# Conditioning of a two-layer trunk: its accumulator moves to a PSUM bank in sets of 512 columns, and its sums over partitions to TensorE and ScalarE

## The chip, the cores and the metric

The kernel runs on one core of a Trainium2 chip. The metric is the device time of one execution in microseconds; before the change it is 2387.78 us, the median of three runs (2386.66 to 2390.29). The profile is of one execution on that core.

## The reference

A trunk of two layers works on 256 tokens of width 2048, in float32. Each layer has a token mixer (layer 0: a gated unit that mixes positions within chunks of 128; layer 1: attention with a forget gate) and a dense layer of hidden width 5632. Each of the four parts gets a shift, a scale and a gate from the condition vector c:

```
c_act = silu(c)
for i in range(DEPTH):
    mod = c_act @ ada_w[i] + ada_b[i]
    sh1, sc1, g1, sh2, sc2, g2 = jnp.split(mod, N_MOD, axis=-1)
    h = modulate(rms_norm(x, norm_mix_g[i]), sh1, sc1)
    ...
    x = x + g1[:, None, :] * y
    h = modulate(rms_norm(x, norm_ffn_g[i]), sh2, sc2)
    x = x + g2[:, None, :] * swiglu_ffn(h, ffn_w_gate[i], ffn_w_up[i], ffn_w_down[i])
```

The product with ada_w, (2, 2048, 6 x 2048), is a vector times a matrix of 201 MB in all: the conditioning, which this change is about.

## The kernel before

Weights come in chunks of 1 MB (4 k-tiles of 128 rows x 512 columns, wchunk) into one of five raw buffers, which the conditioning shares. ScalarE casts half of a chunk to the high part hi (L259), and VectorE or GpSimd subtracts it from raw to give the low part lo (L263). In layer 0 up to the gate and up products every second low part is GpSimd's, later every sixth. TensorE multiplies hi and lo with the split operand, three products for each pair of tiles (mm_a, L300 to L304, for results with channels on partitions; mm_b, L316 to L318, for results by token). VectorE adds partial results from PSUM into SBUF: v at L510, u at L525, the gate and up sums gu at L696, the residual xT at L444.

The conditioning is a product with one row, so VectorE makes it, with ada_w's rows on partitions. A set is 1024 columns: shift and scale of 4 blocks of 128, or 8 blocks of a gate. It comes in 8 chunks of 1 MB (ada_chunk), each of 2 k-tiles; each k-tile is one VectorE step over 1024 columns, acc = raw x cact + acc, with acc in SBUF (L171 for the first, L176 for the other 15):

```
nc.vector.scalar_tensor_tensor(
    out=acc, in0=raw[:, k, :], scalar=cact[:, kt : kt + 1], in1=acc,
    op0=ALU.mult, op1=ALU.add,
)
```

After the eighth chunk ada_sum adds over the 128 partitions. For the six sets of layer 0's mixer TensorE transposes the eight blocks into PSUM (L197) and ScalarE sums each over its row (L203). For the other 18 sets VectorE does it: four transposes within blocks of 32 (L212), four reductions (L213), a product with the matrix fold on TensorE (L218) and four adds into mod (L222). From the scale comes acol (L225), from acol and rstd the operand hA (modulate, L412 to L421).

The order is set in two steps. In the program, pump calls ada_next after each weight chunk at a rate (1.5 to 0.95 in layer 0's mixer, 1.0 and 0.78 up to the gate and up products of the first dense layer, then 0.5), and need calls it until a set that is wanted next is done. From this the tile scheduler fixes the order on each engine when the kernel is built; each engine then takes its instructions in that order. From the dense layers on, a conditioning step also stands behind the last low part but one of VectorE (paced).

PSUM has eight banks: six in the pool psm for the products (banks), two in psx for everything else (misc): transposes, norms, the spatial weights pre, the scores of attention.

Of the kernel before, what the change touches and what calls it, by code (L numbers as in the profile page):

```python
# [8 lines left out]
F32 = mybir.dt.float32  # L9
F32R = mybir.dt.float32r  # L10
AF = mybir.ActivationFunctionType
ALU = mybir.AluOpType
# [4 lines left out]
P = 128  # L17
# [11 lines left out]
# Vectors of the conditioning, in the order of their columns.  # L29
# [4 lines left out]
def trunk_kernel(  # L34
# [107 lines left out]
    ada_v = [ada_w[i].rearrange("(kt p) (v n) -> p kt v n", p=P, n=D) for i in range(2)]  # L142
    # A set is SH and SC of 4 blocks, or 8 blocks of a gate; its product comes in 8 chunks of 1 MB.
    ada_acc = {}
    # The last low parts that VectorE makes; once paced, its part of a chunk goes behind them.
    lo_last, paced = [], []

    def ada_chunk(layer, half, b0, q):
        """Chunk q of 8 of SH and SC of 4 blocks from b0, or of 8 blocks of the gate."""
        raw = rawp.tile([P, 4, 512], F32, tag="raw", name="raw")  # L150
        raw = raw.rearrange("p a b -> p (a b)").rearrange("p (k w) -> p k w", k=2)
        ks = slice(2 * q, 2 * q + 2)
        if b0 < KT:
            for v in range(2):
                nc.sync.dma_start(
                    out=raw[:, :, 512 * v : 512 * v + 512],
                    in_=ada_v[layer][:, ks, 3 * half + v, P * b0 : P * b0 + 512],
                )
        else:
            c0 = P * (b0 - KT)  # L160
            nc.sync.dma_start(out=raw, in_=ada_v[layer][:, ks, 3 * half + 2, c0 : c0 + 1024])
        if q == 0:
            ada_acc[0] = accp.tile([P, 1024], F32, tag="acc", name="acc")
        acc = ada_acc[0]
        for k in range(2):
            kt = 2 * q + k
# [13 lines left out]
        if q == 7:  # L180
            ada_sum(layer, half, b0, acc)

    def ada_sum(layer, half, b0, acc):
        """The sums over the partitions: by TensorE and ScalarE while the loads and VectorE hold
        the time; else within blocks of 32 by the transposing copy, then over the four blocks
        by a product with fold[p, q] = (p = q mod 32)."""
        red = small.tile([P, 32], F32, tag="red", bufs=2, name="red")
        pair = b0 < KT
        key = (layer, half, b0)
        mv = mod[layer].rearrange("p (v n) -> p v n", n=16)[:, 3 * half : 3 * half + 3, :]  # L190
        dst = mv[:, 0:2, b0 : b0 + 4] if pair else mv[:, 2:3, b0 - KT : b0 - KT + 8]
        if key in by_pe:
            for h in range(2):
                pt = misc()
                for b in range(4):
                    bs = slice(P * b, P * b + P)
                    nc.tensor.transpose(  # L197
                        out=pt[:, bs], in_=acc[:, 512 * h + P * b : 512 * h + P * b + P],
                        identity=ident,
                    )  # L200
                for b in range(4):
                    junk = tmp.tile([P, T], F32, tag="t", bufs=5, name="junk")
                    nc.scalar.activation(  # L203
                        out=junk[:, :P], in_=pt[:, P * b : P * b + P], func=AF.Identity,
                        accum_out=red[:, 4 * h + b : 4 * h + b + 1],
                    )
            src = red[:, :8].rearrange("p (v n) -> p v n", v=dst.shape[1])
            nc.vector.tensor_add(out=dst, in0=dst, in1=src)
        else:
            for a in range(4):  # L210
                tr = tmp.tile([P, T], F32, tag="t", bufs=5, name="tr")
                nc.vector.transpose(out=tr, in_=acc[:, T * a : T * a + T])  # L212
                nc.vector.tensor_reduce(  # L213
                    out=red[:, 8 * a : 8 * a + 8],
                    in_=tr.rearrange("p (c i) -> p c i", i=32), axis=AX.X, op=ALU.add,
                )
            pt = misc()[:, :32]
            nc.tensor.matmul(pt, lhsT=fold, rhs=red, start=True, stop=True)  # L218
            src = pt.rearrange("p (v n a) -> p v n a", v=dst.shape[1], a=4)
            for a in range(4):  # L220
                r = slice(32 * a, 32 * a + 32)
                nc.vector.tensor_add(out=dst[r], in0=src[r, :, :, a], in1=dst[r])  # L222
        if pair:
            s = slice(b0, b0 + 4)
            nc.vector.scalar_tensor_tensor(  # L225
                out=acol[layer][half][:, s], in0=mv[:, 1, s], scalar=1.0,
                in1=(gain_mix, gain_ffn)[half][layer][:, s], op0=ALU.add, op1=ALU.mult,
            )
        ready.add(key)

    by_pe = {(0, 0, b) for b in range(0, 32, 4)}
    ready = set()
    ada_todo = [
        (layer, half, b0, q)
        for layer in range(2) for half in range(2) for b0 in (0, 4, 8, 12, KT, KT + 8)
        for q in range(8)
# [13 lines left out]
    def need(layer, half, b0):  # L250
        """The chunks up to the set from k-tile b0 (-1: the gate) are in the program."""
        while (layer, half, b0) not in ready:
            ada_next()

# [12 lines left out]
    # What the splits of the next half chunks don't overtake, and the engine of their low parts.  # L267
# [18 lines left out]
    def mm_a(ps, parts, xs, first, last, fused=True, order="p"):  # L286
        """Transposed results of four blocks, [hi x (hi | lo)] and [lo x hi], or their sum."""
# [20 lines left out]
    def mm_b(ps, parts, xs, first, last, fused=True, order="p"):  # L308
        """Results by token of 512 columns, for the two blocks of tokens."""
# [15 lines left out]
    def proj(  # L325
# [3 lines left out]
        """head: the operand is still being made, by prep if given; tail: the results are waited  # L329
        for; also: other work, by chunk."""  # L330
# [13 lines left out]
    def summed(ps):  # L344
        """hi x hi + lo x hi + hi x lo of a bank, [P, T]."""
        s = tmp.tile([P, T], F32, tag="t", bufs=5, name="us")
        nc.scalar.copy(out=s, in_=ps[:, T:])
        nc.vector.tensor_add(out=s, in0=ps[:, 0:T], in1=s)
        return s

# [14 lines left out]
    def rsqrt(y, ms, n, width):  # L365
        """y = (ms / n + EPS) ** -0.5 with a Newton step after the table's value."""
# [16 lines left out]
    def load_table(func, after):  # L383
        """The table of an activation of a later column, while nothing waits for it."""
        nc.scalar.activation(out=rstd[:, 0:1], in_=after, func=func)

    def norm(sq, stt, square):
        """After the last block of the residual: rstd."""
# [6 lines left out]
    def head_start(first, prep):  # L395
        """The first operand after a norm goes before the splits of the second chunk."""
# [3 lines left out]
    def split_into(dst, src):  # L400
        """src [P, T] as dst = (hi | lo)."""
# [3 lines left out]
    def modulate(h, k0, n, a, sh):  # L405
        """The k-tiles of a chunk, on VectorE in the order written: no wait but the first."""
# [605 lines left out]
```

## Time and profile before

| | |
|---|---|
| median of 3 runs | 2387.78 us (2386.66 to 2390.29) |
| span of the profiled execution, first to last instruction | 2387.4 us |
| TensorE products / weight loads busy | 2250.8 us (94%) / 2030.7 us (85%) |
| VectorE busy | 1829.0 us (77%) |
| ScalarE busy | 1072.8 us (45%) |
| GpSimd busy | 682.2 us (29%) |
| moved from and to HBM | 605.63 MB, mean 254 GB/s |

Of the profiled execution the trace has the span and no other time; it stands 0.4 us below the median. Busy time is the time in which an engine has an instruction at work. A share over the whole span hides that the stages have different limits, so the rows below are read by stage. TensorE's matmuls are pipelined and their ends are modelled, so its busy time is not its rate.

The stages of the program, by TensorE's products in the trace: the first operand is ready at 47 us; layer 0's u and v products to 287 us, its output projection and norm to 409; gate and up of the first six groups of the dense layer to 733, the rest of it to 1205; attention to 1512, its output projection to 1609; gate and up of layer 1 to 1900, the rest to the end.

### The profile page before, as it was taken

The numbers are of one execution on the slowest core, as the hardware profiler recorded it, in microseconds if no ns is written. First come the engines' busy times: TensorE is split into PE (matmuls) and PEld (weight loads), VectorE is DVE, ScalarE is ACT, GpSimd is POOL, SyncE is SP. The second block draws the span as 40 slices with busy tenths as digits, with TensorE's granted clock in tenths as the row PEclk, the third lists the DMA queues.
The fourth block names the chain that finished last, engine by engine and source line by source line (L and its number), as shares of the span: only waits on it lengthen the run. The fifth ranks groups of instructions, "written<-read, shape, count | busy, mean of one in ns | idle before, by whom it ended". The sixth has DMA issues, their size and how long they took to land.

```text
span 2387.4 us, 36384 instructions
## 1 busy us (share of the span) xinstructions
PE 2250.8 (94%) x14333; PEld 2030.7 (85%) x14333; DVE 1829.0 (77%) x2340; ACT 1072.8 (45%) x1609; POOL 682.2 (29%) x385
## 2 busy tenths in 40 slices
PE   5898887999989999999989999999999999999998
PEld 3777777999878888888978888889999988888887
DVE  7899997899997778677688767767798974444464
ACT  4434643533344344544444444445444533444443
POOL 2343354444462111212221121231113511122221
PEclk8999998999999999999999999999999999999999
DMA  9889785978867788788758777667778775555552
GB/s 372 290 275 317 248 313 198 349 282 286 290 237 250 282 285 287 260 296 290 254 178 281 265 261 272 218 241 247 266 268 284 241 261 184 190 191 180 194 177 89
DMA packets 290703, 605.63 MB, mean 254 GB/s; under 512 B 13634, under 2 KB 13762, under 8 KB 290274
## 3 DMA queue, kind: packets, MB, share of 16 engines
q1 hardware_dynamic: 290242, 603.14, 73.1%
q8 instruction: 112, 1.84, 0.3%
q14 instruction: 59, 0.48, 0.1%
q0 software_dynamic: 288, 0.16, 0.0%
q10 hardware_dynamic: 2, 0.01, 0.0%
HBM read 601.15 MB, written 2.11 MB: 253 GB/s over the span
## 4 chain that ended last, share of the span: by engine, by line
PE 71%; DVE 22%; issue 4%; DMA 2%; ACT 1%; POOL 0%; SPq 0%; DVEq 0%; ACTq 0%; POOLq 0%
PE mm L300 30%; PE mm L304 22%; DVE acc L176 8%; PE mm L302 6%; PE mm L303 6%; DVE lo L263 5%; DVE gu L696 2%; PE mm L317 1%; PE mm L318 1%; PE mm L316 1%; DVE hA L421 1%; DVE m L403 1%; DMA raw<-in_ada_w_dram 1%; ACT hi L259 1%; DVE v L510 1%
## 5 line engine op out<-in xcount | busy, mean ns | idle before, releaser
L259 ACT CAST hi<-raw 128x1024 fp32r<-128x1024 f32 x752 | 781.2, 1050 | 906.1 <-PE mm L300 501.4
L263 DVE TENSOR_TENSOR lo<-raw,hi 128x1024 fp32r<-128x1024 f32 x560 | 733.2, 1315 | 373.1 <-ACT hi L259 371.3
L304 PE MATMUL mm<-hA,lo 128*128 128x256 f32 x3584 | 987.2, 285 | 19.8 <-DVE lo L263 19.3
L263 POOL TENSOR_TENSOR lo<-raw,hi 128x1024 fp32r<-128x1024 f32 x192 | 510.6, 2661 | 1345.0 <-ACT hi L259 1228.8
L304 PEld LDWEIGHTS mm<-hA,lo 128*128 128x128 f32 x3584 | 685.3, 193 | 31.8 <-DVE lo L263 22.2
L300 PE MATMUL mm<-hA,hi 128*128 128x512 f32 x1792 | 623.8, 397 | 8.9 <-DVE hA L421 8.9
L176 DVE SCALAR_TENSOR_TENSOR acc<-raw,cact,acc 128x1024 f32<-128x1024 f32 x360 | 553.9, 1539 | 6.4 <-DMA raw<-in_ada_w_dram 3.8
L302 PE MATMUL mm<-hA,hi 128*128 128x256 f32 x1792 | 509.8, 290 | 43.4 <-DVE gu L696 25.4
L303 PE MATMUL mm<-hA,hi 128*128 128x256 f32 x1792 | 510.3, 287 | 0.0
L300 PE MATMUL mm<-m,hi 128*128 128x512 f32 x1248 | 432.9, 397 | 0.0
L300 PEld LDWEIGHTS mm<-hA,hi 128*128 128x128 f32 x1792 | 333.1, 188 | 81.1 <-issue 8.4
L302 PEld LDWEIGHTS mm<-hA,hi 128*128 128x128 f32 x1792 | 348.4, 196 | 52.0 <-DVE gu L696 29.1
L304 PE MATMUL mm<-m,lo 128*128 128x256 f32 x1408 | 382.1, 281 | 2.4 <-DVE lo L263 2.4
L303 PEld LDWEIGHTS mm<-hA,hi 128*128 128x128 f32 x1792 | 352.0, 196 | 0.2
L304 PEld LDWEIGHTS mm<-m,lo 128*128 128x128 f32 x1408 | 266.2, 189 | 8.9 <-DVE lo L263 3.2
L300 PEld LDWEIGHTS mm<-m,hi 128*128 128x128 f32 x1248 | 231.8, 188 | 49.1
L696 DVE TENSOR_TENSOR gu<-mm,gu 128x256 f32<-128x256 f32 x288 | 110.8, 414 | 30.2 <-PE mm L304 29.7
L444 DVE SCALAR_TENSOR_TENSOR xT<-mm,mod,xT 128x256 f32<-128x256 f32 x176 | 75.0, 476 | 48.6 <-PE mm L304 48.6
L317 PE MATMUL mm<-lo,hA 128*128 128x512 f32 x256 | 101.9, 399 | 5.6 <-DVE lo L263 5.6
L316 PE MATMUL mm<-hi,hA 128*128 128x512 f32 x256 | 99.4, 403 | 3.6 <-ACT hA L416 3.6
L318 PE MATMUL mm<-hi,hA 128*128 128x512 f32 x256 | 99.7, 392 | 0.0
L300 PE MATMUL mm<-yB,hi 128*128 128x512 f32 x192 | 70.3, 413 | 8.7 <-DVE xT L444 4.4
(203 smaller groups left out, 1940.2 us busy)
## 6 DMA issues: line engine op xcount, KB each, us to landing
raw<-in_ada_w_dram SPq DMA_DIRECT2D x256, 512.0 KB, 5.1
raw<-in_ffn_w_gate_dram SPq DMA_DIRECT2D x88, 1024.0 KB, 5.6
raw<-in_ffn_w_up_dram SPq DMA_DIRECT2D x88, 1024.0 KB, 5.1
raw<-in_ffn_w_down_dram SPq DMA_DIRECT2D x88, 1024.0 KB, 5.3
raw<-in_ada_w_dram SPq DMA_DIRECT2D x64, 1024.0 KB, 5.2
raw<-in_b_w_in_dram SPq DMA_DIRECT2D x48, 1024.0 KB, 5.4
raw<-in_a_w_in_dram SPq DMA_DIRECT2D x32, 1024.0 KB, 5.4
raw<-in_a_w_out_dram SPq DMA_DIRECT2D x16, 1024.0 KB, 5.6
```

What stands on the lines that cost most here:

```text
L176: nc.vector.scalar_tensor_tensor(out=acc, in0=raw[:, k, :], scalar=cact[:, kt : kt + 1], in1=acc, op0=ALU.mult, op1=ALU.add,)
L259: nc.scalar.copy(out=out_hi, in_=src)
L263: ins = eng.tensor_sub(out=out_lo, in0=src, in1=out_hi.bitcast(F32))
L300: nc.tensor.matmul(ps[j], lhsT=hi[:, js], rhs=x, start=start, stop=False)
L302: nc.tensor.matmul(o, lhsT=hi[:, js], rhs=x[:, 0:T], start=start, stop=False)
L303: nc.tensor.matmul(o, lhsT=hi[:, js], rhs=x[:, T:], start=False, stop=False)
L304: nc.tensor.matmul(o, lhsT=lo[:, js], rhs=x[:, 0:T], start=False, stop=(kt == last))
L316: nc.tensor.matmul(ps[t], lhsT=xh, rhs=hi[:, k, :], start=(kt == first), stop=False)
L317: nc.tensor.matmul(ps[t], lhsT=xh, rhs=lo[:, k, :], start=False, stop=False)
L318: nc.tensor.matmul(ps[t], lhsT=xl, rhs=hi[:, k, :], start=False, stop=(kt == last))
L444: stt = nc.vector.scalar_tensor_tensor(out=xT[:, kt, :], in0=half, scalar=gate[:, kt : kt + 1], in1=xT[:, kt, :], op0=ALU.mult, op1=ALU.add,)
L696: nc.vector.tensor_add(out=dst, in0=ps[j][:, 0:T], in1=dst)
```

## The change

A set is now 512 columns of one vector, in 4 chunks of 1 MB (one transfer each), so there are 48 sets in place of 24 and each k-tile is a step over 512 columns. The accumulator is a bank of misc while in_bank is set, and a tile in SBUF from the forget gate's weights to the end of attention. After the last step ScalarE copies a bank's sums to SBUF (kept), and for every set TensorE transposes four blocks and ScalarE sums them; VectorE adds the four sums to mod. The path by VectorE's transposes and fold is gone. sgu takes its PSUM tile from the product banks. Shift and scale sets of the same blocks follow each other, so a gate or operand waits for the same amount of ada_w as before, and the pump rates are the same. The core of the diff:

```diff
-    def ada_chunk(layer, half, b0, q):
+    def ada_chunk(layer, v, b0, q):
         raw = rawp.tile([P, 4, 512], F32, tag="raw", name="raw")
...
+        nc.sync.dma_start(
+            out=raw, in_=ada_v[layer][:, 4 * q : 4 * q + 4, v, P * b0 : P * b0 + 512]
+        )
         if q == 0:
-            ada_acc[0] = accp.tile([P, 1024], F32, tag="acc", name="acc")
-        acc = ada_acc[0]
-        for k in range(2):
-            kt = 2 * q + k
+            ada_acc[0] = (
+                misc() if in_bank[0] else accp.tile([P, 512], F32, tag="acc", name="acc"),
+                in_bank[0],
+            )
+        acc, banked = ada_acc[0]
+        for k in range(4):
+            kt = 4 * q + k
...
-        if q == 7:
-            ada_sum(layer, half, b0, acc)
+        if q == 3:
+            ada_sum(layer, v, b0, acc, banked)
+
+    def ada_sum(layer, v, b0, acc, banked):
+
+        red = small.tile([P, 4], F32, tag="red", bufs=2, name="red")
+        if banked:
+            kept = accp.tile([P, 512], F32, tag="acc", name="kept")
+            nc.scalar.copy(out=kept, in_=acc)
+            acc = kept
+        pt = misc()
+        for b in range(4):
+            bs = slice(P * b, P * b + P)
+            nc.tensor.transpose(out=pt[:, bs], in_=acc[:, bs], identity=ident)
+        for b in range(4):
+            junk = tmp.tile([P, T], F32, tag="t", bufs=5, name="junk")
+            nc.scalar.activation(
+                out=junk[:, :P], in_=pt[:, P * b : P * b + P], func=AF.Identity,
+                accum_out=red[:, b : b + 1],
+            )
+        dst = mod[layer][:, 16 * v + b0 : 16 * v + b0 + 4]
+        nc.vector.tensor_add(out=dst, in0=dst, in1=red)
...
     def sgu(g0):
-        pt = misc()
+        pt = banks(1)[0]
...
     fsc, wx = forget_weights()
+    in_bank[0] = False
...
+    in_bank[0] = True
     first = out_proj(b_w_out[0].rearrange("(kt p) n -> p kt n", p=P), oB, 1, RATE)
```

How the order moves, at three places. First VectorE in the gate and up products of the first dense layer (gu is the sum of gate and up parts, mm a bank of products), around the end of a set. Before:

```order
L696 TENSOR_TENSOR gu<-mm,gu 128x256 x3
L176 SCALAR_TENSOR_TENSOR acc<-raw,cact,acc 128x1024 x2
L696 TENSOR_TENSOR gu<-mm,gu 128x256
L212 STREAM_TRANSPOSE tr<-acc 128x256
L696 TENSOR_TENSOR gu<-mm,gu 128x256
L263 TENSOR_TENSOR lo<-raw,hi 128x1024
L212 STREAM_TRANSPOSE tr<-acc 128x256 x3
L213 TENSOR_REDUCE red<-tr 128x8
L696 TENSOR_TENSOR gu<-mm,gu 128x256 x2
L213 TENSOR_REDUCE red<-tr 128x8 x2
L171 TENSOR_SCALAR acc<-raw,cact 128x1024
L213 TENSOR_REDUCE red<-tr 128x8
```

And now, with the same adds and low parts (L674 is L696, L241 is L263, L168 and L173 are the conditioning steps):

```order
L674 TENSOR_TENSOR gu<-mm,gu 128x256
L173 SCALAR_TENSOR_TENSOR misc<-raw,cact,misc 128x512
L674 TENSOR_TENSOR gu<-mm,gu 128x256
L241 TENSOR_TENSOR lo<-raw,hi 128x1024
L674 TENSOR_TENSOR gu<-mm,gu 128x256 x3
L168 TENSOR_SCALAR misc<-raw,cact 128x512
L674 TENSOR_TENSOR gu<-mm,gu 128x256
L241 TENSOR_TENSOR lo<-raw,hi 128x1024
L674 TENSOR_TENSOR gu<-mm,gu 128x256
L173 SCALAR_TENSOR_TENSOR misc<-raw,cact,misc 128x512
L674 TENSOR_TENSOR gu<-mm,gu 128x256 x2
L173 SCALAR_TENSOR_TENSOR misc<-raw,cact,misc 128x512
```

The transposes and reductions are gone, and the new set begins in the other bank while the old one waits for its copy; the steps stand singly between adds where pairs stood.

Second, ScalarE in the same stage, where before there were casts and operands only (hi a high part, kept the copy of a bank, junk and red the sums). Now:

```order
L237 CAST hi<-raw 128x1024 x7
L185 COPY kept<-misc 128x512
L237 CAST hi<-raw 128x1024 x3
L193 ACTIVATE junk,red<-misc 128x128 x4
L237 CAST hi<-raw 128x1024
L394 ACTIVATE hA<-xr,mod_130 128x256 x2
```

Each set puts a copy and four sums among the casts, with three casts between the copy and the sums, which wait for TensorE's transposes.

Third, VectorE in layer 0's mixer, where the spatial weights are prepared (pre, which also uses misc; v and u are the sums of the products). Now, from the end of one set to the start of the next:

```order
L173 SCALAR_TENSOR_TENSOR misc<-raw,cact,misc 128x512 x2
L488 TENSOR_TENSOR v<-mm,v 128x512
L241 TENSOR_TENSOR lo<-raw,hi 128x1024
L488 TENSOR_TENSOR v<-mm,v 128x512
L198 TENSOR_TENSOR mod_130<-mod_130,red 128x4
...
L540 SCALAR_TENSOR_TENSOR pre<-misc,ln_cols,pre 128x128 x4
L503 TENSOR_TENSOR u<-mm,u 128x256 x2
L168 TENSOR_SCALAR misc<-raw,cact 128x512
```

No conditioning step stands between, where before the steps went on beside pre; they come later.

## Rows read from the trace of the kernel before

**Rows 1.** The chain that ended last, by engine and by line.

```profile
PE 71%; DVE 22%; issue 4%; DMA 2%; ACT 1%; POOL 0%; SPq 0%; DVEq 0%; ACTq 0%; POOLq 0%
PE mm L300 30%; PE mm L304 22%; DVE acc L176 8%; PE mm L302 6%; PE mm L303 6%; DVE lo L263 5%; DVE gu L696 2%; PE mm L317 1%; PE mm L318 1%; PE mm L316 1%; DVE hA L421 1%; DVE m L403 1%; DMA raw<-in_ada_w_dram 1%; ACT hi L259 1%; DVE v L510 1%
```

**Rows 2.** Busy us by stage: PE, PEld, DVE, ACT, POOL; clock, DMA share, GB/s.

```profile
47.00:287.00 240.00, 211.04 (x1268) 183.32 (x1267) 229.67 (x265) 112.09 (x208) 91.67 (x33) 0.96 0.85 290
287.00:409.00 122.00, 99.63 (x598) 87.90 (x596) 109.19 (x121) 44.26 (x75) 61.98 (x31) 0.92 0.76 259
409.00:733.00 324.00, 298.68 (x2331) 292.86 (x2332) 309.33 (x375) 142.13 (x210) 151.86 (x70) 0.96 0.78 279
733.00:1205.00 472.00, 470.72 (x2765) 413.94 (x2763) 341.89 (x405) 206.60 (x268) 106.35 (x67) 1.00 0.79 275
1617.00:1900.00 283.00, 280.73 (x2317) 279.56 (x2316) 237.73 (x354) 137.32 (x203) 67.58 (x36) 1.00 0.76 261
```

**Rows 3.** The same view of L176 on VectorE alone, four stages.

```profile
47.00:287.00 240.00, 106.92 (x65) 0.96 0.85 290
287.00:409.00 122.00, 53.74 (x26) 0.92 0.76 259
409.00:733.00 324.00, 132.28 (x72) 0.96 0.78 279
733.00:1205.00 472.00, 96.38 (x74) 1.00 0.79 275
```

**Rows 4.** VectorE's groups over the span: count, busy us, mean ns, idle before.

```profile
L263 DVE TENSOR_TENSOR lo<-raw,hi 128x1024 fp32r<-128x1024 f32 x560 | 733.2, 1315 | 373.1 <-ACT hi L259 371.3 <-PE mm L304 0.7
L176 DVE SCALAR_TENSOR_TENSOR acc<-raw,cact,acc 128x1024 f32<-128x1024 f32 x360 | 553.9, 1539 | 6.4 <-DMA raw<-in_ada_w_dram 3.8
L696 DVE TENSOR_TENSOR gu<-mm,gu 128x256 f32<-128x256 f32 x288 | 110.8, 414 | 30.2 <-PE mm L304 29.7
L444 DVE SCALAR_TENSOR_TENSOR xT<-mm,mod,xT 128x256 f32<-128x256 f32 x176 | 75.0, 476 | 48.6 <-PE mm L304 48.6
...
L171 DVE TENSOR_SCALAR acc<-raw,cact 128x1024 f32<-128x1024 f32 x24 | 27.2, 1133 | 0.0
L212 DVE STREAM_TRANSPOSE tr<-acc 128x256 f32<-128x256 f32 x72 | 26.4, 413 | 0.1
L213 DVE TENSOR_REDUCE red<-tr 128x8 f32<-128x256 f32 x72 | 26.0, 401 | 0.0
L510 DVE TENSOR_TENSOR v<-mm,v 128x512 f32<-128x512 f32 x32 | 21.1, 679 | 0.1
...
L222 DVE TENSOR_TENSOR mod<-misc,mod 32x8 f32<-32x8 f32 x72 | 11.5, 160 | 1.3 <-PE misc L218 0.6
```

**Rows 5.** Instructions of the tile acc: shortest, median and longest ns.

```profile
L176 DVE SCALAR_TENSOR_TENSOR acc<-raw,cact,acc x360: 1256/1279/3527, 14.3 to 1928.6; 128x1024 f32<-128x1024 f32 x180
```

**Rows 6.** Timeline of VectorE from 575 us: start, us taken, instructions merged.

```profile
575.08 1.07 DVE L696 TENSOR_TENSOR gu<-mm,gu 128x256 f32<-128x256 f32 x3
576.07 3.75 DVE L176 SCALAR_TENSOR_TENSOR acc<-raw,cact,acc 128x1024 f32<-128x1024 f32 x2
...
580.07 1.22 DVE L263 TENSOR_TENSOR lo<-raw,hi 128x1024 fp32r<-128x1024 f32 x1
```

**Rows 7.** Timeline of GpSimd in the same microseconds.

```profile
574.22 3.19 POOL L263 TENSOR_TENSOR lo<-raw,hi 128x1024 fp32r<-128x1024 f32 x1 [3.14 <-ACT hi L259]
```

**Rows 8.** Timeline of TensorE around eight transposes in the output projection.

```profile
333.18 0.28 PE L304 MATMUL mm<-yB,lo 128*128 128x256 f32 x1
333.30 1.03 PE L197 MATMUL misc<-ident,acc 128*128 128x128 f32 x8
334.09 0.47 PE L300 MATMUL mm<-yB,hi 128*128 128x512 f32 x1
```

**Rows 9.** ScalarE's groups over the span, two of them.

```profile
L203 ACT ACTIVATE junk<-misc 128x128 f32<-128x128 f32 x48 | 12.6, 292 | 6.4 <-PE misc L197 6.4
...
L917 ACT COPY vf<-mm 128x512 f32<-128x512 f32 x8 | 4.7, 582 | 2.4 <-PE mm L318 2.4
```

More of the change, by code (lines that the diff above doesn't have):

```diff
@@ L144, in trunk_kernel @@
     ada_acc = {}
+    in_bank = [True]
     lo_last, paced = [], []
-    def ada_chunk(layer, half, b0, q):
+    def ada_chunk(layer, v, b0, q):
         raw = rawp.tile([P, 4, 512], F32, tag="raw", name="raw")
[L151 to L161, printed above, removed]
-        if q == 0:
-            ada_acc[0] = accp.tile([P, 1024], F32, tag="acc", name="acc")
-        acc = ada_acc[0]
-        for k in range(2):
-            kt = 2 * q + k
+        nc.sync.dma_start(
+            out=raw, in_=ada_v[layer][:, 4 * q : 4 * q + 4, v, P * b0 : P * b0 + 512]
+        )
+        if q == 0:
+            ada_acc[0] = (
[5 more added lines that the diff above has]
+            kt = 4 * q + k
             with ExitStack() as order:
@@ L179, in ada_chunk @@
                     )
-        if q == 7:
-            ada_sum(layer, half, b0, acc)
[L183 to L193, printed above, removed]
-                pt = misc()
[L195 to L223, printed above, removed]
@@ new lines, in ada_chunk @@
+        if q == 3:
[18 more added lines that the diff above has]
+        nc.vector.tensor_add(out=dst, in0=dst, in1=red)
+        half, what = divmod(v, 3)
+        if what == 1:
@@ L224, in ada_sum @@
             s = slice(b0, b0 + 4)
             nc.vector.scalar_tensor_tensor(
-                out=acol[layer][half][:, s], in0=mv[:, 1, s], scalar=1.0,
+                out=acol[layer][half][:, s], in0=dst, scalar=1.0,
                 in1=(gain_mix, gain_ffn)[half][layer][:, s], op0=ALU.add, op1=ALU.mult,
             )
-        ready.add(key)
-    by_pe = {(0, 0, b) for b in range(0, 32, 4)}
+        ready.add((layer, v, b0))
     ready = set()
     ada_todo = [
-        (layer, half, b0, q)
-        for layer in range(2) for half in range(2) for b0 in (0, 4, 8, 12, KT, KT + 8)
-        for q in range(8)
+        (layer, v, b0, q)
@@ L237, in trunk_kernel @@
+        for layer in range(2) for half in range(2)
+        for v, b0 in [(3 * half + w, b) for b in range(0, KT, 4) for w in range(2)]
+        + [(3 * half + 2, b) for b in range(0, KT, 4)]
+        for q in range(4)
     ]
@@ L248, in pump, with need @@
             ada_next()
-    def need(layer, half, b0):
-        while (layer, half, b0) not in ready:
+    def need(layer, v, b0):
+        while (layer, v, b0) not in ready:
             ada_next()
@@ L431, in prep @@
             n = 4
-            need(layer, half, k)
+            need(layer, 3 * half + 1, k)
             return modulate(h, k, n, acol[layer][half], vec(layer, SH1 + 3 * half))
@@ L599, in sgu @@
     def sgu(g0):
-        pt = misc()
+        pt = banks(1)[0]
         for g in range(g0, g0 + 2):
@@ L651, in out_proj @@
             )
-            need(layer, 0, KT + 8)
+            need(layer, G1, 12)
             done = residual(ps, 512 * cg, vec(layer, G1), True, not end)
@@ L731, in ffn @@
                 )
-                need(layer, 1, KT + 8)
+                need(layer, G2, 12)
                 done = residual(ps, 512 * cg, vec(layer, G2), pi == 1, not end)
```

## The prediction

> **What bounds the kernel now.** I read the chain of waits first: 71% of it is TensorE and 22% VectorE, and VectorE's largest line is the conditioning step L176 with 8% [rows 1]. So neither engine bounds the whole, and the next view has to be by stage. The busy time by stage [rows 2] shows where each holds: from 47 to 287 us (the u and v products of layer 0) VectorE is busy 229.67 of 240 us and TensorE 211; from 409 to 733 us (gate and up of the first dense layer) VectorE 309.33 of 324 and TensorE 298.68 at a mean granted clock of 0.96, nearly always at the level of 2.4 GHz; from 733 to 1205 us TensorE 470.72 of 472. The same gate and up work in layer 1, 1617 to 1900 us, has fewer conditioning steps beside it: VectorE is busy 237.73, TensorE 280.73, and it takes 283 us, not 324. VectorE is what is paid for in the first 733 us, TensorE after it.
>
> Then the steps by line: L176 costs 1539 ns in the mean [rows 4], but its median is 1279 and its longest 3527 [rows 5], and in the first three stages the means are 106.92 / 65 = 1.64, 53.74 / 26 = 2.07 and 132.28 / 72 = 1.84 us, against 96.38 / 74 = 1.30 after 733 us [rows 3]. What stretches them is seen at 574 us: GpSimd runs a low part from 574.22 to 577.41 [rows 7]; in that time three adds whose first operand is in PSUM pass at full speed, 1.07 us for three, and the two L176 that follow take 3.75 us, not 2.6 [rows 6]. An L176 reads raw and acc, two tensors in SBUF, and so does GpSimd's step; the VectorE step stands still until GpSimd ends. The steps with one operand in PSUM show no such thing: L444 and L510 average 476 and 679 ns over the kernel [rows 4], as much as any of them should take. GpSimd is busy 91.67 of the 240 us and 151.86 of the 324 [rows 2], so this happens often.
>
> **The change part by part.** *The step itself.* Each L176 of 1024 columns becomes two of 512, with the accumulator in PSUM while in_bank is set. Its form, one operand in SBUF, one in PSUM, the result into PSUM, is nowhere in the trace. The nearest rows: the add of 512 columns with one operand in PSUM, 679 ns (L510); and what the scalar column adds, 476 for L444 against 414 for L696 at 256 columns, 62 ns [rows 4]. I take 679 + 62 = 741 ns. From below it is 679; from above, if reading and writing one bank halves the rate, as long as 1024 columns of SBUF, 1279 [rows 5]. I take the value near the lower end since L444 has the same operands and the same scalar and differs in the place of the result only. Two steps are then 1.48 us: more than 1.28 without GpSimd, less than the 1.64 to 2.07 measured up to 733 us. The first step of a set, L171, 1133 ns with GpSimd's stalls in it [rows 4], becomes two that read no second tensor, at most 679 each; I count no change.
>
> A rule stands against this. The adds of 256 and 512 columns give (679 - 414) / 256 = 1.035 ns a column and so 149 ns that do not depend on it; the undisturbed L263 of 1024 columns in SBUF, 1.22 us [rows 6], gives 160 ns. By these rows an operand in PSUM costs nothing extra. The Trainium skill, Perfetto Trace Analysis, section on optimizing Scalar/DVE operations, puts about 60 ns of overhead on a VectorE instruction in SBUF and about 125 in PSUM, and advises larger operations. By it the 182 new steps before 409 us would cost 65 ns more each, 12 us, and the sum below would be some 2362; no run here shows that form.
>
> *47 to 287 us.* 65 steps, 106.92 us, become 130 x 0.741 = 96.3: 10.6 less. The 32 low parts, the operands hA and xr still read two SBUF tensors and meet GpSimd as before; DMA at a share of 0.85 [rows 2] leaves room for this much. I take -10.
>
> *287 to 409 us.* 26 steps, 53.74 us, become 52 x 0.741 = 38.5: 15 less, and one set's sum on VectorE, 4 x (413 + 401 + 160) ns = 3.9 us [rows 4], goes. TensorE is busy 99.63 of 122 us here, and the norm at the end is a chain of its own. I take -7.
>
> *409 to 733 us.* 72 steps, 132.28 us, become 144 x 0.741 = 106.7: 25.6 less. Four sums by VectorE, 4 x 3.9 = 15.6 us, become small adds of 128x4, which at 0.16 us come to about 2. VectorE falls from 309 to some 270 us and is no longer the bound. The bound is then TensorE: layer 1 does the same products in 283 us [rows 2]. Transposes add 10 sets x 0.4 = 4 us (below), and VectorE at 270 of 290 us will still be late at times: I take 296, so -28.
>
> *TensorE after 733 us.* The sums of all sets now go through four transposes. Eight of them between two products of a saturated stretch moved the next product from 333.18 + 0.11 to 334.09 us [rows 8]: 0.8 us, so 0.4 for four. Of 360 steps 65 + 26 + 72 lie in the three stages [rows 3, 4] and 15, the first set's, before them; the other 182 are 12 sets, 24 of the new ones: 24 x 0.4 = 9.6, less the 12 fold products that go (about 0.2 us each), is +7. The gate and up stage of layer 1 may win 1 us from VectorE; I take +6.
>
> *Hidden.* ScalarE gets a copy of 512 columns (582 ns) and four sums (292 ns and a read of the accumulator) for each set [rows 9]; it is busy less than half of each stage [rows 2]. After 733 us the steps are dearer, 74 of them 96.38 us against 148 x 0.741 = 109.7, and in attention, with the accumulator in SBUF, likewise; VectorE has 130 us free of 472 there [rows 2]. If that cover went, it would cost these 13 us. On SP's queue each two transfers of 512 KB become one of 1 MB, and the gates' rows are halved to 2 KB; the bytes are the same. The accumulator holds one of the two misc banks; sgu moves to the other pool, and while the spatial weights use misc the order starts no new set, which puts work off without stopping VectorE.
>
> *The start.* The first operand needs two sets: 32 x 0.741 = 23.7 us against 16 x 1.28 = 20.5, less a shorter tail of four sums: +2.
>
> The sum: +2 - 10 - 7 - 28 + 6 = -37. The profiled execution has a span of 2387.4 us, 0.4 below the median of the runs, 2387.78, so no correction is due: 2350 us. At the lower price, 0.679, another 10 us go before 409 us: 2340.
>
> **The rivals.** *Transfers become the bound.* The stages up to 733 us already move 259 to 290 GB/s at shares of 0.76 to 0.85 [rows 2]; in 296 us instead of 324 the third would need a share of 0.85. For: five raw buffers give little room ahead. Against: the share has room on average. If the first stage wins nothing, the second 4 and the third 14 us: 2387.4 + 2 - 4 - 14 + 6 = 2377.
>
> *The stall moves on.* The low parts, operands and products m still read two SBUF tensors. If GpSimd stops them for all the time that it now stops L176, the new steps only show their higher price: 130 x 0.741 - 65 x 1.28 = +13 us in the first stage, 52 x 0.741 - 26 x 1.28 - 3 = +2 in the second, 144 x 0.741 - 72 x 1.28 - 14 = +1 in the third, and 2387.4 + 2 + 13 + 2 + 1 + 6 = 2411. On a line between this, +24, and the sum, -37, no change lies at 0.6 of the stalls passed on. For: GpSimd's steps are as many as before. Against: most of VectorE's steps between two low parts will have an operand in PSUM and pass while GpSimd works [rows 6, 7].
>
> *TensorE waits at the hand-over, slower.* Every set now goes VectorE, ScalarE's copy, TensorE, ScalarE, VectorE, and TensorE takes its queue in order. If the four transposes stand before the copy is done, behind one cast of 1.05 us on ScalarE, TensorE waits 1.05 + 0.58 = 1.63 us, 48 times: 78 us, and the time is 2387.4 - 37 + 78 = 2428. It decides from 37 / 48 = 0.77 us per set on. For: ScalarE has casts on both sides of the copy. Against: casts lie between the copy and the sums in the order, so room is left, and TensorE is the last engine after 733 us.
>
> *The bank reads and writes at half rate, slower.* At 1279 ns the first stage needs 229.7 - 106.9 + 166.3 = 289 us of VectorE, 49 more than there is, the second 10, the third 25: about 2471.
>
> **How the numbers follow.** Forecast 0.63; transfers 0.15; the stall moves on 0.10; hand-over 0.07; half rate 0.05. A measurement tells about 0.2%, 4.8 us, from no change, 2383 to 2392.6. Faster is 0.63 + 0.15 = 0.78; of the stall that moves on in large part about half, 0.05, falls near no change, and 0.05 + 0.07 + 0.05 = 0.17 is slower. The forecast alone spans 2326 to 2370: its lower end lets the first stage win 20 (DMA at 0.93) and the third 41 us (to 283), and the upper halves the first three terms. The range is 2326 to 2387: it takes in transfers and the near half of the stall that moves on; the 0.17 of slower cases and a little below are left out.
>
> **What would show it.** Right: the step of 512 columns at 720 to 760 ns with a longest near its median in the first 733 us; gate and up of layer 0 ending in under 300 us, with TensorE's clock at 1.00 there; 733 to the end longer by 4 to 9 us. Wrong: a step over 850 ns; TensorE idle before the transposes by more than 0.5 us per set; L263's mean rising by over 0.5 us in the first stages.

## The result, and the profile after

The changed kernel takes 2402.25 us, the median of four runs (2399.42 to 2405.62), against 2389.03 for the kernel before (2386.66 to 2393.24) on the same chip. The ratio is 1.0053, with a 95% interval of 1.0036 to 1.0071: slower by half a per cent, where the forecast was 2350 and faster. The range, 2326 to 2387, does not hold the time.

The profiled execution has a span of 2399.8 us against 2387.4. I cut both at the first product of TensorE in each stage. (The stage limits of the prediction lie up to 7 us beside these first products: 47 against 44.2, 1205 against 1211.9. This shifts its windows and not the differences below. First products of "48" or "56" us in the expectations are read with 3 us too many, as the 47 is.)

| us | before | after | difference | forecast |
|---|---|---|---|---|
| start to the first product | 44.2 | 65.6 | +21.4 | +2 |
| u and v products | 241.1 | 259.0 | +17.9 | -10 |
| output projection and norm | 124.4 | 115.2 | -9.2 | -7 |
| gate and up, layer 0 | 320.1 | 294.2 | -25.9 | -28 |
| rest of the first dense layer | 482.1 | 485.6 | +3.5 | } |
| attention | 297.2 | 308.6 | +11.4 | } +6 |
| output projection, layer 1 | 105.3 | 104.7 | -0.6 | } |
| gate and up, layer 1, and the end | 773.1 | 766.9 | -6.2 | } |

The chain that ended last, by engine and by line, beside [rows 1]: VectorE's part fell from 22% to 12%, and its conditioning step from 8% to 4%.

```profile
PE 81%; DVE 12%; DMA 3%; issue 2%; ACT 2%; POOL 0%; DVEq 0%; ACTq 0%; POOLq 0%
PE mm L278 32%; PE mm L282 24%; PE mm L280 8%; PE mm L281 8%; DVE misc L173 4%; DVE lo L241 2%; DMA raw<-in_a_w_in_dram 2%; PE mm L296 2%; PE mm L294 2%; PE mm L295 2%; DVE gu L674 1%; ACT hi L237 1%; PE misc L190 1%; DVE xr L390 1%; DVE m L381 1%
```

Busy time by stage, the first four stages (columns as in [rows 2]):

```profile
68.00:327.00 259.00, 221.61 (x1293) 192.28 (x1292) 219.61 (x340) 117.49 (x226) 84.67 (x33) 0.91 0.80 275
327.00:442.00 115.00, 96.72 (x590) 84.81 (x589) 96.85 (x139) 46.49 (x89) 54.30 (x30) 0.95 0.74 260
442.00:737.00 295.00, 287.60 (x2349) 284.10 (x2348) 262.45 (x399) 151.44 (x284) 136.74 (x67) 0.99 0.87 300
737.00:1222.00 485.00, 476.92 (x2803) 419.48 (x2802) 357.62 (x452) 225.93 (x366) 104.98 (x71) 0.99 0.79 273
```

L173 on VectorE alone in two of them, as in [rows 3]:

```profile
68.00:327.00 259.00, 97.24 (x130) 0.91 0.80 275
...
442.00:737.00 295.00, 104.16 (x139) 0.99 0.87 300
```

The third row is what was forecast: VectorE no longer holds gate and up, and TensorE is busy 287.60 of 295 us. The first row is not: VectorE is busy 219.61 of 259 us, so it has 39 us free in a stage that became longer, DMA moves less, and TensorE's granted clock falls from 0.96 to 0.91. The steps are not to blame, as their groups show (columns as in [rows 4]):

```profile
L241 DVE TENSOR_TENSOR lo<-raw,hi 128x1024 fp32r<-128x1024 f32 x560 | 728.0, 1305 | 397.6 <-ACT hi L237 394.5
L173 DVE SCALAR_TENSOR_TENSOR misc<-raw,cact,misc 128x512 f32<-128x512 f32 x630 | 472.9, 751 | 11.2 <-DMA raw<-in_ada_w_dram 2.9
...
L173 DVE SCALAR_TENSOR_TENSOR acc<-raw,cact,acc 128x512 f32<-128x512 f32 x90 | 75.4, 838 | 0.8
...
L168 DVE TENSOR_SCALAR misc<-raw,cact 128x512 f32<-128x512 f32 x42 | 31.4, 748 | 17.7 <-ACT v L478 10.8 <-ACT kept L185 3.5 <-ACT pre L535 3.5
L198 DVE TENSOR_TENSOR mod<-mod,red 128x4 f32<-128x4 f32 x48 | 26.7, 557 | 11.0 <-ACT junk L193 10.6
```

The step in a bank takes 751 ns. The low part L241 has the mean of L263 [rows 4], so the stalls were not passed on to it. But L168, the first step of a set, waits for three things that are no data of its own: v (the bias), kept (a set's copy) and pre (the spatial weights). All are releases of misc tiles. The timeline of VectorE at the start:

```profile
33.33 1.23 DVE L241 TENSOR_TENSOR lo<-raw,hi 128x1024 fp32r<-128x1024 f32 x1 [4.21 <-ACT hi L237]
45.37 0.75 DVE L168 TENSOR_SCALAR misc<-raw,cact 128x512 f32<-128x512 f32 x1 [10.82 <-ACT v L478]
46.16 7.88 DVE L173 SCALAR_TENSOR_TENSOR misc<-raw,cact,misc 128x512 f32<-128x512 f32 x10
```

The first operand needs a shift set and a scale set. The second set's accumulator is allocated, in the program, behind 12 misc tiles: eight for x transposed and four for the bias of v. VectorE stands still for 10.82 us until ScalarE has read the last but one of them, at 45.3 us: of two banks the last tile holds one, and the accumulator takes the other. In the u and v products the 12 tiles of pre do the same, and the steps thin out (L173 alone, around pre):

```profile
100.00:119.00 19.00, 11.10 (x15) 1.00 0.95 332
119.00:164.00 45.00, 3.76 (x5) 0.96 0.58 193
164.00:200.00 36.00, 18.76 (x25) 0.81 0.78 264
```

Five steps in 45 us. DMA falls from a share of 0.95 to 0.58, and behind it, from 164 to 200 us, TensorE is busy 25.68 of 36 us, at a granted clock of 0.81. I read this as follows: chunks whose steps are put off keep the raw buffers, which the weights share. Two rows of the stage's wait lists bear on it (us in total, times, longest): the transfer of a weight chunk is held until a conditioning step has passed, and ScalarE's cast waits for the chunk.

```profile
SPq L250 <- DVE misc L173: 65.4, 20, 11.9
ACT hi L237 <- DMA raw<-in_a_w_in_dram: 63.2, 16, 10.4
```

Before, the longest of the first was 6.8 us (66.3 in total), and the second was 18.4 us in 5. So the first did not grow in sum; single waits became longer. The experiments test where the accumulator's place comes in; the number of raw buffers was not varied.

### The profile page after: what moved, and what is told of

Read it like the earlier page. It is cut to its first block, busy times and chain, and to the rows that moved or that the text cites. A ratio compares the mean times of both kernels' runs of the same rounds, so it can differ in the third digit from the quotient of the medians.

```text
span 2399.8 us, 36985 instructions
## 1 busy us (share of the span) xinstructions
PE 2257.2 (94%) x14441; PEld 2037.9 (85%) x14441; DVE 1775.1 (74%) x2550; ACT 1130.1 (47%) x1939; POOL 633.1 (26%) x385
## 4 chain that ended last, share of the span: by engine, by line
PE 81%; DVE 12%; DMA 3%; issue 2%; ACT 2%; POOL 0%; DVEq 0%; ACTq 0%; POOLq 0%
PE mm L278 32%; PE mm L282 24%; PE mm L280 8%; PE mm L281 8%; DVE misc L173 4%; DVE lo L241 2%; DMA raw<-in_a_w_in_dram 2%; PE mm L296 2%; PE mm L294 2%; PE mm L295 2%; DVE gu L674 1%; ACT hi L237 1%; PE misc L190 1%; DVE xr L390 1%; DVE m L381 1%
## 5 line engine op out<-in xcount | busy, mean ns | idle before, releaser
L241 DVE TENSOR_TENSOR lo<-raw,hi 128x1024 fp32r<-128x1024 f32 x560 | 728.0, 1305 | 397.6 <-ACT hi L237 394.5
L241 POOL TENSOR_TENSOR lo<-raw,hi 128x1024 fp32r<-128x1024 f32 x192 | 481.7, 2510 | 1378.0 <-ACT hi L237 1336.8
L173 DVE SCALAR_TENSOR_TENSOR misc<-raw,cact,misc 128x512 f32<-128x512 f32 x630 | 472.9, 751 | 11.2 <-DMA raw<-in_ada_w_dram 2.9
L674 DVE TENSOR_TENSOR gu<-mm,gu 128x256 f32<-128x256 f32 x288 | 113.8, 417 | 29.8 <-PE mm L282 29.4
L173 DVE SCALAR_TENSOR_TENSOR acc<-raw,cact,acc 128x512 f32<-128x512 f32 x90 | 75.4, 838 | 0.8
```

The lines of the kernel that those rows point to most:

```text
L173: nc.vector.scalar_tensor_tensor(out=acc, in0=raw[:, k, :], scalar=cact[:, kt : kt + 1], in1=acc, op0=ALU.mult, op1=ALU.add,)
L241: ins = eng.tensor_sub(out=out_lo, in0=src, in1=out_hi.bitcast(F32))
L674: nc.vector.tensor_add(out=dst, in0=ps[j][:, 0:T], in1=dst)
```

## The experiments

Theory A: the accumulator's wait among the misc tiles costs the start and the u and v products, while the step in a bank wins where VectorE binds. Rival B: the sets of 512 columns and their hand-over through ScalarE and TensorE cost it, wherever the accumulator lies. Stages below are the table's.

**All accumulators in SBUF.**

```diff
-    in_bank = [True]
+    in_bank = [False]
...
-    in_bank[0] = True
     first = out_proj(b_w_out[0]...
```

> Every accumulator stays in SBUF; sets of 512 columns and the sums by TensorE and ScalarE stay as changed. Theory A (the changed kernel loses at the start and in the u and v products because an accumulator must wait for one of the two misc banks, and wins in gate and up because the step in a bank is not stopped by GpSimd): the first product comes near 48 us again, not 66; the u and v products take 240 to 250 us, not 259; gate and up of layer 0 goes back to 305 to 320 us from 294, with the 512-column steps at over 0.9 us in the mean there; the time is 2385 to 2395. Rival B (the loss is from the sets of 512 and their hand-over through ScalarE and TensorE): first product near 65 us, u and v near 259, time 2410 or more.

Measured: 2431.05 us, ratio 1.0161 (1.0147 to 1.0174). The first product comes at 53.3 instead of 65.6; u and v take 255.8, gate and up 327.9. Neither theory had it whole, and the time is B's. The start gives back 12 of 21 us, more than half of what A says, but u and v stay long, since VectorE is now the bound there (busy 251.85 of 256 us). Its step in gate and up, VectorE's costliest group there:

```profile
L173 DVE SCALAR_TENSOR_TENSOR acc<-raw,cact,acc 128x512 f32<-128x512 f32 x140 | 155.4, 1111 | 4.2 <-DMA raw<-in_ada_w_dram 2.2
```

**In SBUF up to the output projection, in a bank from there on.**

```diff
-    in_bank = [True]
+    in_bank = [False]
...
+    in_bank[0] = True
     first = out_proj(a_w_out[0]...
```

> Accumulators in SBUF up to the end of layer 0's u and v products, in a bank from its output projection on as changed. Theory A: first product near 48 us, u and v 240 to 250 us, gate and up of layer 0 still 294 to 298 us; time 2368 to 2378, faster than both kernels. Rival B: first product near 65, u and v near 259, time 2400 to 2405.

Measured: 2382.33 us, 0.9955 (0.9943 to 0.9967), faster than both kernels. Gate and up takes 293.9 us, 34 less than in the run above, with the same sets and the same sums:

```profile
L173 DVE SCALAR_TENSOR_TENSOR misc<-raw,cact,misc 128x512 f32<-128x512 f32 x139 | 104.0, 748 | 4.0 <-DMA raw<-in_ada_w_dram 2.7
```

Only the accumulator's place differs, and with it ScalarE's copy of the bank: 1111 ns against 748. This shows the gain that the forecast rested on. First product 53.6, u and v 256.6 where A wanted 240 to 250, and so the time misses A's 2368 to 2378.

**The start's 12 tiles from the product banks** (L457, L473).

```diff
-        pt = misc()
+        pt = banks(1)[0]
```

> Accumulators in banks as changed; only the 12 tiles of the start that take x transposed and the bias of v are taken from the pool of six product banks, idle then, so that the second set need not wait for them. Theory A: the first step of the second set starts near 30 us, not at 45.4; first product at 48 to 52 us; u and v unchanged at some 259 us; time near 2385. Rival B: first product still near 65 us, time 2400 to 2405.

Measured: 2390.7 us, 0.9994 (0.9983 to 1.0005). The first product comes at 59.5 us, 6 earlier and not 17: the 10.82 us are gone, but now the first set starts at 20.7 us and not at 12.0. TensorE makes the tables' transpose (L122) at 19.1 us instead of 9.1, behind all products of x and the bias, and VectorE's copy of the tables cols (L123), ahead of the first set in the order of both kernels, waits 15.4 us for it. u and v unchanged at 258.2.

**The 12 tiles of pre from the product banks as well** (L525, L533, L536, the same edit).

> As the run before, and the 12 tiles of the spatial weights are taken from the product banks too, so that new sets start while they pass. Theory A: u and v products fall from 259 to 235 to 248 us, since VectorE does not stand idle beside pre; the product banks are in use, so TensorE may wait some us for them; time 2362 to 2375. Rival B: u and v stay near 259 and the time near that of the run before.

Measured: 2361.3 us, 0.9865 (0.9852 to 0.9878). u and v fall from 258.2 to 230.3 us. In the same stretch there are 24 steps where there were 5, and DMA and clock hold:

```profile
95.00:120.00 25.00, 9.84 (x14) 1.00 0.96 331
120.00:165.00 45.00, 17.40 (x24) 1.00 0.90 316
165.00:200.00 35.00, 16.34 (x23) 1.00 0.86 303
```

This is A's half in u and v, and it was the larger one: 28 us for twelve tiles. Rival B is out there: sets and hand-over are the same. But pre itself also passes earlier (its last step L540 at 123.8 us, not 163.8), so that the larger pool might be the gain by itself; the control and the last run below answer that.

**The sets of the start in SBUF, pre in product banks, all later sets as changed.**

```diff
-    in_bank = [True]
+    in_bank = [False]
...
     prep(0)
+    in_bank[0] = True
     for k0, nk in ((0, 4), (4, 4), (8, 4), (12, 4)):
```

> The sets that start before the first operand is made keep their accumulator in SBUF, the spatial weights pass through the product banks, all later sets as changed. Theory A says that the first accumulator waits behind the tiles of the tables and the second behind those of x, both only because it is a misc tile: first product at 56 us, as with everything in SBUF, not at 63; u and v still near 227 us; time 2353 to 2357 (2361.3 less 6.8). Rival (what is left of the start is the 512-column steps and sums, wherever they are): first product stays at 62 to 63 and the time at 2361.

Measured: 2359.73 us, 0.9865 (0.9851 to 0.9879). The first product comes at 50.3, 10 us earlier than in the run before, but the ratio is the same, and the time misses the 2353 to 2357: output projection and norm take 114.3 instead of 109.0. TensorE waits there 8.0 us for VectorE's low parts, 1.0 in the run before; why they come late I have not traced.

**Attention's sums by VectorE and fold again**, on the kernel with both groups of tiles moved.

```diff
+        if by_fold[0]:
+            for a in range(2):
+                tr = tmp.tile([P, T], F32, tag="t", bufs=5, name="tr")
+                nc.vector.transpose(out=tr, in_=acc[:, T * a : T * a + T])
+                nc.vector.tensor_reduce(...)
+            nc.tensor.matmul(pt, lhsT=fold, rhs=red, start=True, stop=True)
...
     in_bank[0] = False
+    by_fold[0] = True
```

> The kernel with x, the bias and the spatial weights in product banks, and in attention the sums over partitions again by VectorE and one product with fold, with sets of 512 in SBUF as changed. Theory S (attention lost 11 us because the sums' transposes and ScalarE's sums stand ahead of the evictions of qk at the head groups' ends): attention falls from 310 to 298 to 302 us, no idle of TensorE at the end of the second head group; time 2349 to 2354. Rival Z (the 512-column steps in SBUF, 1.49 us a k-tile instead of 1.28, cause it): attention stays at 308 to 312, time 2358 to 2363.

Measured: 2349.11 us, 0.9825 (0.9811 to 0.9838). Attention takes 296.2 us instead of 310.0, as S says, and TensorE is busy 296.00 of 296 us. What it was in the changed kernel is seen on TensorE, at the end of the second head group:

```profile
1333.18 0.66 PE L190 MATMUL misc<-ident,acc 128*128 128x128 f32 x4
1335.80 0.70 PE L278 MATMUL mm<-hA,hi 128*128 128x512 f32 x1 [1.96 <-DVE qk L878]
```

The sums' transposes, ScalarE's four sums and VectorE's small add (L198) stand ahead of the eviction of qk (L877, L878), and the next products wait for that bank. With the waits before it TensorE is busy 15.37 of 20 us there, at a granted clock of 0.83:

```profile
1320.00:1340.00 20.00, 15.37 (x72) 12.76 (x71) 5.42 (x15) 5.71 (x25) 3.15 (x4) 0.83 0.33 116
```

This spot is 4.6 of the 11.4 us. The run also takes away the transposes of six sets, 2.4 us at the prediction's 0.4 a set; what the rest hangs on is not shown spot by spot.

**Both of these, and the first chunks written behind the square root of x's norm.**

```diff
-    for q in range(4):
-        ada_next()
...
     rsqrt(x_rs, x_ss, D, NB)
+    for q in range(4):
+        ada_next()
```

> Both of the runs before, and the first chunks' steps written behind the square root of x's norm, so that VectorE's four small steps for it come ahead of the first set, as in the kernel before. If each of the three losses has its own cause: first product at 50 to 53 us, u and v 227, attention 298 to 302; time 2340 to 2347. If the start does not hang on the square root: first product at 56 and time near 2347; with rival Z in attention 10 us more.

Measured: 2344.38 us, 0.9802 (0.9789 to 0.9816). First product 49.3, u and v 231.3, attention 296.7. The square root is worth 1 us at most. What is left of the start, 5 us against before, is mostly the steps: there are 30 of 0.75 us and two of 0.48, each with 0.04 behind it, 24.7 us, against 16 that take 15 x 1.32 + 0.79 = 20.6 in the kernel before.

**The kernel before, all sums by TensorE and ScalarE.**

```diff
-        if key in by_pe:
+        if True:
```

> The kernel before with one edit: the sums of all sets go by TensorE and ScalarE (four transposes of 512 columns twice a set), sets of 1024 columns in SBUF as before. Theory S: attention rises from 297 to 305 us or more, as in all kernels with such sums there; gate and up of layer 0 gains 4 to 13 us, since four sums leave VectorE; time 2385 to 2392. Rival Z: attention stays at 297 to 299; time 2376 to 2384.

Measured: 2382.02 us, 0.9964 (0.9951 to 0.9976). Attention 303.6, gate and up 308.4. So the sums alone give 11.7 of the 25.9 us in gate and up. In attention they cost 6.4 of the 11.4; this kernel hands over half as many sets there. The time is Z's; attention lies between Z's 299 and S's 305, nearer to S. From here to the run with all accumulators in SBUF, which has the same path of sums but sets of 512, gate and up rises from 308.4 to 327.9: in this stage the halved sets alone cost 19.5 us, and the bank's 34 pay for them.

**Control: the kernel before with the same tiles from the product banks** (the edits of the third and fourth run).

> The kernel before, its accumulators in SBUF, with one edit: the tiles of x transposed, of the bias and of the spatial weights come from the product banks. If these tiles cost only where an accumulator waits for a misc bank, nothing is gained here: first product 46 to 48 us, u and v 238 to 243, time 2383 to 2392. If passing them through the larger pool is a gain by itself (they follow each other faster, or stand elsewhere in the order), u and v fall by 10 us or more, time 2365 to 2378, and the gain of the runs above is not the accumulator's.

Measured: 2384.79 us, 0.9983 (0.9974 to 0.9992): 0.2%. First product 43.7, u and v 246.3, longer and not shorter. So moving the tiles is no gain by itself in these stages; it is one where accumulators share misc.

**The fastest kernel, with SBUF accumulators and fold from the end of gate and up on.**

```diff
         n_split[1] = 6
+        if layer == 0:
+            in_bank[0], by_fold[0] = False, True
```

> The fastest kernel so far, and from the end of gate and up of layer 0 to the end of attention accumulators in SBUF and sums by VectorE and fold. If the 3.5 us that the rest of the first dense layer took longer (482.1 to 485.7) are the transposes of the sums on TensorE, it falls to 482 to 483 us and the time to 2339 to 2343; if they are not, it stays at 485 to 486 and the time at 2344.

Measured: 2339.99 us, 0.9798 (0.9785 to 0.9812), which cannot be told from 0.9802. The rest of the first dense layer takes 484.2 us: 1.4 of the 3.5 come back, what the other 2 are stays open.

**A third misc bank, one of the products' six gone; and the same for the kernel before.**

```diff
-    psm = ctx.enter_context(tc.tile_pool(name="psm", bufs=6, space=PSUM))
-    psx = ctx.enter_context(tc.tile_pool(name="psx", bufs=2, space=PSUM))
+    psm = ctx.enter_context(tc.tile_pool(name="psm", bufs=5, space=PSUM))
+    psx = ctx.enter_context(tc.tile_pool(name="psx", bufs=3, space=PSUM))
```

> The changed kernel, nothing moved, but one bank more for misc and one fewer for the products. Theory A (an accumulator waits for a free misc bank): first product at 50 to 63 us instead of 68; u and v 232 to 245 us instead of 259; what the products lose by five banks is what the next run shows; without that loss the time would be 2365 to 2380. Rival B (the pool is not what the steps wait for): first product at 65 or later, u and v near 259.

> The control: the kernel before with the same split of the banks, three for misc and five for products. Its accumulators are in SBUF, so by theory A nothing is gained at the start or in u and v (47 and 241 us, within 3); any time over 2390 is the price of the lost product bank. If u and v fall by 10 us here too, the third bank's gain is not the accumulator's.

Measured: 2395.24 us, 1.0021 (1.0012 to 1.0030), and 2413.16 us, 1.0096 (1.0081 to 1.0111). The first product stays at 64.4 us, where A wanted 50 to 63; u and v fall to 247.8, 3 above A's range, and the control's by 2 only (239.0). VectorE at the start, with three banks:

```profile
44.22 0.75 DVE L168 TENSOR_SCALAR misc<-raw,cact 128x512 f32<-128x512 f32 x1 [9.61 <-ACT v L478]
```

The wait is nearly the same, and again a copy of the bias ends it: that of the second bias tile, at 44.2 us, where with two banks it was the third's, at 45.3. One bank more lets the accumulator start one tile earlier. At the start it is not the number of banks.

**A bank of the accumulators' own**, two for misc, five for products.

```diff
+    psa = ctx.enter_context(tc.tile_pool(name="psa", bufs=1, space=PSUM))
...
-                misc() if in_bank[0] else accp...
+                psa.tile([P, 512], F32, tag="abank", name="abank") if in_bank[0] else accp...
```

> The changed kernel with a bank of its own for the accumulators, two for misc as changed and five for the products. The third misc bank left the second set's first step at 47.0 us. Theory A1 (the wait is for the accumulator's place in the rotation of the misc tiles, behind 12 tiles written before it, whatever the number of banks): with its own bank that step starts at 27 to 30 us, first product at 53 to 57 us, u and v 225 to 236 us; the products pay for the fifth bank some 3 us in the norm after the output projection and 7 in the rest of the first dense layer, as in the control; time 2372 to 2382. Theory A2 (three banks are too few): first product at 65 or later, as with the third misc bank, u and v 245 or more, time 2393 or more.

Measured: 2385.71 us, 0.9979 (0.9968 to 0.9990). First product 50.1, u and v 233.0, with x, the bias and pre still in misc. The second set's first step, there L169:

```profile
25.45 0.76 DVE L169 TENSOR_SCALAR abank<-raw,cact 128x512 f32<-128x512 f32 x1 [0.33 <-ACT kept L186]
```

It starts 20 us earlier than in the changed kernel. As many banks in all as with the third misc bank, but outside the pool: A1 holds, the accumulator waited for its turn among the misc tiles. From 120 to 165 us there are 22 steps, with pre in misc from 109 to 144 us. The time misses the range by 4 us: gate and up takes 303.6, where TensorE waits 14.9 us for the adds gu (7.2 in the changed kernel) and VectorE's low parts take 84.9 us (70.2); attention takes 314.0, though the run with the third misc bank, with five product banks too, had 307.6. What of this the lost product bank costs, and what the single accumulator bank, stays open.

## Why the prediction was wrong

**The price of the step held.** 741 ns was forecast from the nearest rows, 751 measured, with a longest of 758 over 630, while GpSimd ran or not. Over the kernel the low parts and the operands took no more stalls (L241, L399 and L390 805.4 us, before 809.6), so *the stall moves on* and *half rate* are out. The Trainium skill's figures, about 60 and 125 ns of overhead in SBUF and PSUM (Perfetto Trace Analysis, section on optimizing Scalar/DVE operations), would, as an estimate, have set the bank some 65 ns above SBUF. For this form the trace doesn't agree: the median in gate and up is 752 in SBUF and 747 in a bank, at 512 columns both (shortest, median and longest ns, in the first and in the second run above).

```profile
L173 DVE SCALAR_TENSOR_TENSOR acc<-raw,cact,acc x139: 734/752/2939, 433.5 to 749.4; 128x512 f32<-128x512 f32 x139
L173 DVE SCALAR_TENSOR_TENSOR misc<-raw,cact,misc x138: 737/747/757, 423.3 to 710.8; 128x512 f32<-128x512 f32 x138
```

All the signs that the prediction named for being right came out: the step at 751 ns, gate and up at 294.2 us with a granted clock of 0.99, and the end 8.1 us longer. None of them looked at the start or at u and v.

**Transfers** did not become the bound: gate and up ran at a DMA share of 0.87, and u and v, with the tiles of pre moved, at 0.90 from 120 to 165 us without a loss.

**What GpSimd does was right.** With sets and sums the same, 1111 against 748 ns and 34 us in one stage. The Trainium skill, SBUF — State Buffer, section Who interferes with whom, says that a VectorE instruction with two SBUF inputs contends with a GpSimd one that reads SBUF, and one with at most one such input, outside the modes that use two ports, doesn't; these two rows agree. The exception may be at work here: the first step of a set, with one SBUF input, took 1395 ns in the mean of 9 in gate and up where it wrote to SBUF, and 745 where it wrote to a bank.

**Output projection and gate and up: right**, -9.2 and -25.9 for -7 and -28. Of the second, 11.7 is the sums' part.

**u and v: the step that failed** is the sentence that the accumulator holds one of the two misc banks and that this "puts work off without stopping VectorE". Work put off keeps raw buffers, which the weights need: a reading, with the wait rows above for it. Forecast -10, measured +17.9; with the tiles of pre out of the pool it is -10.8, with a bank of its own -8.1. So the -10 was about the right price of the steps, and the putting off, 28.7 us, was priced at nothing.

**The start: the same fault.** It was priced by steps alone, +2; the 12 tiles of x and the bias were not counted at all, although the two sets and these tiles stood in the code, on one pool. Measured +21.4; with a bank of its own +5.9. The +2 itself was 4 short: twice as many steps, with the 0.04 us behind each, are 4.7 us more and not 3.2, and what the shorter tail was to give did not come.

Had both come out as forecast, the span would be 2399.8 - 19.4 - 27.9 = 2352.5.

**After 733 us** the sum was nearly right, +8.1 for +6, by luck and not by its steps: attention lost 11.4, as far as the runs show mostly by the place of the sums in the order, where 24 x 0.4 us of transposes were forecast for all stages together, and the end of the kernel won 6.2 where 1 was counted.

**The hand-over as a rival** priced TensorE's wait before the transposes at 1.63 us a set, 78 in all. The wait list of TensorE over the whole changed kernel (us in total, times, longest) has it three times for 48 sets:

```profile
PE misc L190 <- ACT kept L185: 32.2, 3, 14.7
```

That is 0.67 us a set, over the 0.5 that the prediction named as a sign of being wrong, but not in every set. Two of the three, 28.2 us, stand before the first product, where TensorE waits for the first two sets to be made; the third is 4.0 us in u and v. What it cost elsewhere was not a wait before the transposes but, in attention, one behind them: the eviction.

**Two sums of the prediction** are off, and nothing hangs on them: by its own rows half rate would bring VectorE to 118 of 122 us in the second stage, so that its 10 us there fall away (2461, not 2471), and the forecast with its three gains halved comes to 2373, not 2370.

## What to carry to other kernels

An accumulator that lives for a whole set does not belong in a small rotating pool beside short-lived tiles: it waits for its turn behind every tile that the program allocates before it, and a larger pool need not help, while a buffer of its own, or moving the others, does. A step that is "only put off" is free only if nothing that it holds is wanted by others; here, as I read it, it was the raw buffers, and the loss showed as a lower DMA share and granted TensorE clock, not as VectorE's busy time. And a gain found in one stage should be switched on in that stage first: in_bank from the output projection on alone was faster than both kernels, before any repair.

## What the runs showed of the hardware that was not expected

The first step of a set, one SBUF tensor times a column, took 748 ns into a bank (42 of them) and 506 into SBUF (6). I had taken at most 679.

```profile
L168 DVE TENSOR_SCALAR acc<-raw,cact 128x512 f32<-128x512 f32 x6 | 3.0, 506 | 0.0
```

Here the bank costs 242 ns, though the step with two tensors costs nothing extra. It looks like a rate and not a fixed price: into SBUF the median is 481 ns for 512 columns and 748 for the 1024 of the kernel before (L171), 0.52 ns a column, half of the 1.035 that the prediction found for the adds. That is an estimate from two sizes; no run has a second size into a bank. All first steps together took 34.4 us of VectorE, before 27.2, where no change was counted.

And the add of four columns into mod (L198), all in SBUF, has a mean of 557 ns over 48 where 160 were expected [rows 4]. The timelines of VectorE and GpSimd show one of them in gate and up:

```profile
531.68 1.43 DVE L198 TENSOR_TENSOR mod<-mod,red 128x4 f32<-128x4 f32 x1 [0.34 <-ACT junk L193]
533.03 1.53 DVE L173 SCALAR_TENSOR_TENSOR misc<-raw,cact,misc 128x512 f32<-128x512 f32 x2
```

```profile
530.69 2.40 POOL L241 TENSOR_TENSOR lo<-raw,hi 128x1024 fp32r<-128x1024 f32 x1 [3.35 <-ACT hi L237]
```

It ends with GpSimd's low part, at 533.1 us: here an instruction of four columns waited until GpSimd was done, as the steps of the kernel before did.
